# Gate and up tiles 6 to 21 of a feed-forward layer in pairs, by seven half-size products

## The chip, the cores and the metric

The kernel runs on one core of a Trainium2 chip. The metric is the device time of one execution in microseconds; the runs shown are whole executions, the profile is one more of them, with every instruction recorded.

A core has five engines that run their own queues in order and wait for one another by semaphores: PE (TensorE, matmuls; its weight loads are listed as PEld), DVE (VectorE), ACT (ScalarE), POOL (GpSimd) and SP (SyncE, which issues most DMAs here).

## The reference

Two transformer blocks in float32, one after the other, 512 tokens of width 1024. The change lies in the feed-forward layer that ends the first block:

```
h = rms_norm(x, pre_ffn_norm)
f = (silu(h @ w_ffn_gate) * (h @ w_ffn_up)) @ w_ffn_down     # 1024 -> 2816 -> 1024
x = x + rms_norm(f, post_ffn_norm)
```

## The kernel before

Activations are held transposed: a tile has 128 features as partitions and 512 tokens as columns. The width 1024 is 8 tiles (KD), the inner width 2816 is 22 (KF); `n` numbers these 22. The weights `w_fgu` hold the gate and the up tile of each n one after the other, so row 2n is gate n and row 2n + 1 is up n; each row is 128 x 1024: 8 blocks of 128 columns, one for each k of the contraction.

float32 products are made of three matmuls in float32r. `pair` splits a tile into a high part (ACT, L135, a cast) and a low part (DVE, L139, what the cast lost), and `mm3` (L207 to L209) multiplies high by high, high by low and low by high into one PSUM bank. `wload` has SP load 128 x 1024 of weights into a buffer of a ring (`RAW`, names `wr`; three buffers) and makes two pairs of 512 columns of it (`wh`, `wl`). `lin` is one output tile: 8 k times `mm3`, 24 matmuls of 512 columns. `evac` (L370, DVE) takes the bank to SBUF and multiplies it by R, the reciprocal norm of each token, since `hs` holds the tokens times the gain, not yet normed. `repair` is `pair` of a tile that is then let go (`prh`, `prl`).

SBUF tiles come from 84 slots of 128 x 512 (and 14 half slots). `A` takes the slot at the head of a line of free slots and `free` puts one at its end: a slot that is taken late after it was let go costs no wait, and what a new tile waits for is the last reader of the slot's former tile.

The loop over n: the gate and up tiles of n = 0 to 2 are made by `first_halves` while the norm is still being made; from n = 3 on by two `lin` each. Then silu on the gate tile (ACT), the product with the up tile (DVE, L924) and `repair` of it, whose pair goes into the list `hid`. After n = 10 the down projection of these 11 tiles is made into `fs` (8 tiles, `fs_first`), and after n = 21 `down_last` adds that of the other 11: 6 output tiles by `lin` with 11 k, the last two by `last_halves`, in two halves of 256 columns, so that the norm of the first half can begin while the second half is multiplied.

The kernel is written as one program for all engines; a scheduler orders the instructions of each engine's queue at build time, by its own estimate of times and with the slots as constraints. So the order on each engine is not the order of the source.

Of the kernel before, what the change touches and what calls it, by code (L numbers as in the profile page):

```python
# [10 lines left out]
F32 = mybir.dt.float32  # L11
# [3 lines left out]
ALU = mybir.AluOpType  # L15
# [43 lines left out]
def two_blocks(ctx: ExitStack, tc: tile.TileContext, d, dbg=None):  # L59
    nc = tc.nc  # L60
    V, S, G, PE = nc.vector, nc.scalar, nc.gpsimd, nc.tensor

    NSLOT, NHALF = 84, 14
    cst = ctx.enter_context(tc.tile_pool(name="cst", bufs=1))
    ar = ctx.enter_context(tc.tile_pool(name="ar", bufs=1))
    pp = ctx.enter_context(tc.tile_pool(name="pp", bufs=1, space=bass.MemoryType.PSUM))
# [8 lines left out]
    def A(name, dt=F32, cols=T):  # L75
        if cols > 256 or len(spare_half) < 3:
            i = spare.popleft()
            low[0] = min(low[0], len(spare))
            ap = ar.tile([P, T], dt, tag="slot%d" % i, name=name)[:, :cols]
            owner[id(ap)] = (spare, i, ap, name)  # L80
        else:
            i = spare_half.popleft()
            ap = ar.tile([P, 256], dt, tag="half%d" % i, name=name)[:, :cols]
            owner[id(ap)] = (spare_half, i, ap, name)
        return ap

    def free(*xs):
        for x in xs:
            if isinstance(x, (tuple, list)):
                free(*x)  # L90
            else:
                home, i = owner.pop(id(x))[:2]
                home.append(i)

    def ring(pool, n, shape, name, dt=F32):
        tiles = [pool.tile(shape, dt, name="%s%d" % (name, i)) for i in range(n)]
        at = [0]

# [17 lines left out]

    MM, AT, OP, ST = (lambda: bank("mm")), (lambda: bank("at")), (lambda: bank("op")), (lambda: bank("st"))
    share(mm=(0, 1, 2, 3, 4), at=(5, 6), op=(7,), st=(5, 6))
    RAW = ring(ar, 3, [P, 1024], "wr")
    SMALL = ring(cst, 32, [P, 8], "sm")  # L120
    RTOK = ring(cst, 16, [P, NT], "rtok")

# [82 lines left out]
    def mm3(ps, a, b, first, last):  # L205
        (ah, al), (bh, bl) = a, b
        r = PE.matmul(ps, lhsT=ah, rhs=bh, start=first, stop=False)  # L207
        PE.matmul(ps, lhsT=ah, rhs=bl, start=False, stop=False)  # L208
        PE.matmul(ps, lhsT=al, rhs=bh, start=False, stop=last)  # L209
        return r.ins  # L210

    def lin(w, n, hs, cols=T, k0=0, after=None):

        kt = len(hs)
        ps = MM()
        wt = wtile(w, n, kt, k0)
        for k in range(kt):
            r = mm3(ps[:, :cols], wpart(wt, k), hs[k], k == 0, k == kt - 1)
            if k == 0 and after:
                order(r, after)  # L220
        free(wt[1])
        return ps
# [114 lines left out]
    def vcol(name, i=0, n=1):  # L337
        return vec[:, VOFF[name] + i:VOFF[name] + i + n]
# [28 lines left out]
    def evac(ps, name, Rt, scale=None, cols=T):  # L367
        o = A(name)
        if scale is None:
            V.tensor_tensor(o[:, :cols], ps[:, :cols], Rt[:, :cols], ALU.mult)  # L370
        else:
            V.scalar_tensor_tensor(o[:, :cols], ps[:, :cols], scale, Rt[:, :cols], ALU.mult, ALU.mult)
        return o

    def repair(x, cols=T, eh=None, el=None):

        p = pair("pr", x[:, :cols], None, cols, eh, el)
        free(x)
        return p

    HALVES = (slice(0, 256), slice(256, 512))

    def last_halves(ns, wts, hs, out, after=None, stat=None, at=(0, 0)):

# [521 lines left out]
    def fs_first(n, ps):  # L908
        fs[n] = A("f")
        S.copy(fs[n], ps)  # L910
# [4 lines left out]
        V.tensor_tensor(fs[n][:, c], fs[n][:, c], ps, ALU.add)  # L915
        st.add(fs[n][:, c], c)

    for n in range(KF):
        if n < 3:
            zg, zu = firsts[2 * n], firsts[2 * n + 1]  # L920
        else:
            zg, zu = [evac(lin(d["w_fgu"], 2 * n + j, hs), "z", R) for j in range(2)]
        act("silu", zg, zg, AF.Silu)
        V.tensor_tensor(zu, zu, zg, ALU.mult)  # L924
        free(zg)
        hid.append(repair(zu))
        if n == HF - 1:
            for m in range(KD):
                fs_first(m, lin(d["w_fd"], m, hid))
            free(hid)  # L930
            hid = []
    free(hs, R)

    def down_last(w, hid, out, after, ahead=None, nl=2, stat=None, at=(0, 0)):
        for n in range(KD - nl):
            both(out)(n, lin(w, n, hid, k0=HF))
        wl2 = [wtile(w, n, KF - HF, HF) for n in range(KD - nl, KD)]
        if ahead:
            ahead()
        last_halves(range(KD - nl, KD), wl2, hid, out, after, stat, at)  # L940
        free(hid)
# [5 lines left out]
            v2ws.extend(wload(d["w2V"][0, :, k * T:(k + 2) * T]))  # L947
        qkws.extend(wtile(d["w2T"], n, KD) for n in (0, 4))

    down_last(d["w_fd"], hid, fs_add, st.done, ahead, 2, st, (5, 14))  # L950
    hs, sth = chained(xs, "attn_norm", DM, post_norm(fs, st, "post_ffn", xs))


# [550 lines left out]
```

## Time and profile before

| | |
|---|---|
| three runs | 1758.90, 1757.07, 1757.78 us (median 1757.78) |
| profiled execution | 1757.92 us; span of its instructions 1755.9 us |
| granted TensorE clock, mean | 0.994 |
| busy in the span | PE 98%, PEld 84%, DVE 61%, ACT 47%, POOL 5% |
| DMA | 169.97 MB, 97 GB/s on average |

A row of groups reads: line, engine, operation, output<-inputs, shapes, count | busy us, mean ns of one | idle time of the engine just before them, and what ended most of it. A row of the timeline reads: start in us from the span's start, length in us, engine, line, operation; "x4" merges four that follow each other, and [..] is the idle time before, with what ended it. Matmuls, DVE and ACT instructions overlap at their ends, so what one costs in a full queue is the distance between starts, which is shorter than its length. DMA rows give KB each and the median us from issue to landing.

### The profile page before, as it was taken

To read this page: it belongs to the slowest core of one execution; us is meant where nothing else is said; L and a number is where in the kernel's file an instruction comes from. 1 tells how busy PE (TensorE), PEld (TensorE's weight loads), DVE (VectorE), ACT (ScalarE), POOL (GpSimd) and SP (SyncE) were. 2 spreads that over 40 slices of the span, in tenths; PEclk is the share of its full clock that TensorE was granted. 3 is DMA by queue.
4 is the path that set the end of the run, shared out by engine and by line. 5 is a ranking of instruction groups with operands and counts; after the bars stand their busy time and mean duration, and the time that the engine had idled before them with its cause. 6 is when DMAs were issued, how large, how long until landed. Compare 5 with 4: busy or idle time off the path is not lost.

```text
span 1755.9 us, 24063 instructions
## 1 busy us (share of the span) xinstructions
PE 1718.4 (98%) x9039; PEld 1469.4 (84%) x9039; DVE 1079.4 (61%) x2103; ACT 830.9 (47%) x1695; POOL 90.5 (5%) x109
## 2 busy tenths in 40 slices
PE   8999999999999999999999999999999999999998
PEld 7888888878889888888897887887898988888887
DVE  7447863587757543344557656787756587547752
ACT  6534543565544432323425656687525454324442
POOL 1000000100004000000012000000210200000000
PEclk9999999999999999999999999999999999999999
DMA  6212251223440423422413443433314133432221
GB/s 225 83 48 72 83 162 41 61 61 104 156 156 5 152 79 90 120 77 81 146 46 95 121 109 103 126 102 108 128 44 137 47 102 88 126 96 84 74 83 49
DMA packets 60915, 169.97 MB, mean 97 GB/s; under 512 B 7616, under 2 KB 16512, under 8 KB 60800
## 3 DMA queue, kind: packets, MB, share of 16 engines
q1 hardware_dynamic: 60528, 168.24, 32.1%
q8 instruction: 71, 1.16, 0.3%
q14 instruction: 44, 0.36, 0.1%
q10 hardware_dynamic: 144, 0.14, 0.0%
q0 software_dynamic: 128, 0.07, 0.0%
HBM read 151.64 MB, written 2.10 MB: 88 GB/s over the span
## 4 chain that ended last, share of the span: by engine, by line
PE 87%; DVE 5%; ACT 3%; DMA 2%; issue 2%; POOL 1%; SPq 0%; POOLq 0%; DVEq 0%; ACTq 0%
PE bank L207 27%; PE bank L208 27%; PE bank L209 27%; PE bank L1086 1%; DVE wl L139 1%; DVE hl L141 1%; PE bank L729 1%; DVE f L861 1%; DMA wr<-w_mq 1%; PE bank L1045 0%; ACT wh L135 0%; PE bank L1046 0%; DVE x L862 0%; PE bank L293 0%; DMA mem<-memT 0%
## 5 line engine op out<-in xcount | busy, mean ns | idle before, releaser
L139 DVE TENSOR_TENSOR wl<-wr,wh 128x512 fp32r<-128x512 f32 (+2 forms) x568 | 375.6, 678 | 302.5 <-ACT wh L135 171.2
L135 ACT CAST wh<-wr 128x512 fp32r<-128x512 f32 (+2 forms) x568 | 333.9, 608 | 462.8 <-PE bank L209 144.6
L207 PE MATMUL bank<-hh,wh 128*128 128x512 f32 (+1 forms) x1380 | 504.9, 368 | 7.5 <-ACT wh L135 5.7
L209 PE MATMUL bank<-hh,wl 128*128 128x512 f32 (+1 forms) x1380 | 505.3, 367 | 0.0
L208 PE MATMUL bank<-hl,wh 128*128 128x512 f32 (+1 forms) x1380 | 504.7, 366 | 0.0
L207 PEld LDWEIGHTS bank<-hh,wh 128*128 128x128 f32 x1380 | 260.6, 189 | 48.8 <-ACT wh L135 6.4
L209 PEld LDWEIGHTS bank<-hh,wl 128*128 128x128 f32 x1380 | 260.7, 189 | 41.7 <-DVE wl L139 0.7
L208 PEld LDWEIGHTS bank<-hl,wh 128*128 128x128 f32 x1380 | 260.8, 189 | 40.5
L208 PE MATMUL bank<-prl,wh 128*128 128x512 f32 (+1 forms) x471 | 171.5, 364 | 0.0
L209 PE MATMUL bank<-prh,wl 128*128 128x512 f32 (+1 forms) x471 | 171.4, 364 | 0.0
L207 PE MATMUL bank<-prh,wh 128*128 128x512 f32 (+1 forms) x471 | 171.1, 365 | 0.0
L207 PEld LDWEIGHTS bank<-prh,wh 128*128 128x128 f32 x471 | 88.8, 189 | 14.2
L208 PEld LDWEIGHTS bank<-prl,wh 128*128 128x128 f32 x471 | 88.9, 189 | 14.1
L209 PEld LDWEIGHTS bank<-prh,wl 128*128 128x128 f32 x471 | 88.8, 189 | 13.9
L254 POOL TENSOR_TENSOR rtok<-sm,minus_half 128x2 f32<-128x2 f32 (+1 forms) x20 | 16.4, 822 | 1271.4 <-DVE sm L253 1271.4
L208 PE MATMUL bank<-wl,hh 128*128 128x512 f32 (+1 forms) x192 | 71.4, 374 | 0.4 <-DVE wl L139 0.4
L209 PE MATMUL bank<-wh,hl 128*128 128x512 f32 (+1 forms) x192 | 70.3, 374 | 0.0
L207 PE MATMUL bank<-wh,hh 128*128 128x512 f32 (+1 forms) x192 | 69.6, 377 | 0.0
L270 ACT ACTIVATE sq<-x 128x256 f32<-128x256 f32 (+1 forms) x88 | 36.8, 425 | 42.2 <-DVE x L1332 38.4
L137 ACT ACTIVATE hh<-x,vec 128x256 fp32r<-128x256 f32 (+1 forms) x72 | 37.7, 527 | 36.4 <-DVE x L862 14.1
L281 POOL TENSOR_TENSOR sq<-sq 128x256 f32<-128x256 f32 x56 | 46.1, 827 | 95.1 <-ACT sq L270 92.7
L141 DVE SCALAR_TENSOR_TENSOR hl<-x,vec,hh 128x256 fp32r<-128x256 f32 (+1 forms) x72 | 46.2, 658 | 5.4 <-ACT hh L137 5.4
(368 smaller groups left out, 2761.9 us busy)
## 6 DMA issues: line engine op xcount, KB each, us to landing
wr<-w_fgu SPq DMA_DIRECT2D x44, 512.0 KB, 3.7
wr<-w_up SPq DMA_DIRECT2D x44, 512.0 KB, 3.6
wr<-w1T SPq DMA_DIRECT2D x16, 512.0 KB, 3.5
wr<-w_gate SPq DMA_DIRECT2D x16, 512.0 KB, 3.8
wr<-w_fd SPq DMA_DIRECT2D x16, 512.0 KB, 3.6
wr<-w2T SPq DMA_DIRECT2D x16, 512.0 KB, 3.9
wr<-w_dn SPq DMA_DIRECT2D x16, 512.0 KB, 3.6
wr<-w1K SPq DMA_DIRECT2D x12, 512.0 KB, 4.3
```

What stands on the lines that cost most here:

```text
L135: r = S.copy(hi, src) if eh is S else V.tensor_copy(hi, src)
L137: r = S.activation(hi, src, AF.Copy, scale=scale)
L139: q = el.tensor_tensor(lo, src, f(hi), ALU.subtract)
L141: q = V.scalar_tensor_tensor(lo, src, scale, f(hi), ALU.mult, ALU.subtract)
L207: r = PE.matmul(ps, lhsT=ah, rhs=bh, start=first, stop=False)
L208: PE.matmul(ps, lhsT=ah, rhs=bl, start=False, stop=False)
L209: PE.matmul(ps, lhsT=al, rhs=bh, start=False, stop=last)
L270: S.activation(q[:, :w], src, AF.Square)
L281: self.eadd.tensor_tensor(acc, acc, q[:, :w], ALU.add)
L729: PE.transpose(tp[:, i * P:(i + 1) * P], ps_tiles[i][:, b * P:(b + 1) * P], C("ident"))
L861: r = V.scalar_tensor_tensor(fs[k][:, c], fs[k][:, c], vcol(gain, k), st.R[:, c], ALU.mult, ALU.mult)
L1086: PE.matmul(z[:, (b2 - b) * P:w], lhsT=lt, rhs=part[:, :T - b2 * P], start=False, stop=False)
```

## The change

Tiles n = 0 to 5 stay as they are. From n = 6 on, two n are taken together: the two gate tiles by one call of `seven`, then the two up tiles by another, 16 calls in all. A call sees the two tiles of weights as a 2 x 2 block matrix (output tile a or b, first or second 4 k), and the tokens as 2 x 2 blocks too (first or second 4 k, first or second 256 columns), and makes the four blocks of the output from 7 products of half size in place of 8: each product is 4 k times `mm3` on 256 columns, 12 matmuls. In the order of the program the seven stationary operands are a11, a12, s2, s3, s1, s4 and a22, with sums of blocks of weights s1 = a22 + a21, s3 = a11 + a21 (by the blocks' names in the code), s2 = s1 + a11, s4 = s2 + a12; they are called product 1 to 7 below. s2 and s4 are made by DVE. s1 and s3 are made by DMA: SP loads one block into a slot `s`, and POOL issues a DMA that adds the other block to it.

The combinations of token blocks (`ts`) are made once, by `normed_sums`, from tokens that are already normed (`ns`), which are therefore made anew; `hs` and R are let go. The results of the products are joined by DVE: u2, u3, u4 (L290 of the new kernel) and four writes into the two output tiles (L1035), all of 256 columns; u1 is copied by ACT. `evac` is not needed there.

The down projection goes in three passes: after n = 5 (6 k), after n = 13 (8 k, with 8 additions on DVE), and `down_last` (8 k), whose last three tiles go in halves. The ring RAW has four buffers, and there are 82 slots. During the calls all 8 PSUM banks go round.

```diff
-    NSLOT, NHALF = 84, 14
+    NSLOT, NHALF = 82, 14
...
-    RAW = ring(ar, 3, [P, 1024], "wr")
+    RAW = ring(ar, 4, [P, 1024], "wr")
...
+    def seven_sums(b0, b1):
+
+        h0, h1 = HALVES
+        u, v = A("t12"), A("t34")
+        V.tensor_tensor(u[:, h0], b0[:, h1], b0[:, h0], ALU.subtract)
+        V.tensor_tensor(u[:, h1], b1[:, h1], u[:, h0], ALU.subtract)
+        V.tensor_tensor(v[:, h0], b0[:, h1], b1[:, h1], ALU.subtract)
+        V.tensor_tensor(v[:, h1], b1[:, h0], u[:, h1], ALU.subtract)
+        return repair(u), repair(v)
+
+    def seven(w, na, nb, hs, ts, out):
+        half = len(hs) // 2
+        n_ = half * P
+        h0, h1 = HALVES
+        raws = []
+        for n in (na, nb):
+            raw = RAW()
+            nc.sync.dma_start(raw[:, :2 * n_], w[n, :, 0:2 * n_])
+            raws += [raw[:, :n_], raw[:, n_:2 * n_]]
+        a11, a12, a21, a22 = raws
...
+        def ps_for(a, b):
+            ps = MM()
+            for k in range(half):
+                mm3(ps[:, :256], (a[0][:, k * P:(k + 1) * P], a[1][:, k * P:(k + 1) * P]), b(k),
+                    k == 0, k == half - 1)
+            free(a)
+            return ps[:, :256]
+
+        def plus(ps, x, op=ALU.add):
+            o = A("u", F32, 256)
+            V.tensor_tensor(o[:, :256], ps, x[:, :256], op)
+            return o
+
+        def summed(x, y, op):
+            o = A("s", F32, n_)
+            V.tensor_tensor(o[:, :n_], x, y, op)
+            return o
+
+        sums = []
+        for n, c, m, e in ((nb, slice(n_, 2 * n_), nb, slice(0, n_)), (na, slice(0, n_), nb, slice(0, n_))):
+            o = A("s", F32, n_)
+            nc.sync.dma_start(o[:, :n_], w[n, :, c])
+            G.dma_start(o[:, :n_], w[m, :, e], accum_op=ALU.add)
+            sums.append(o)
+        s1, s3 = sums
+        s2 = summed(s1[:, :n_], a11, ALU.add)
+        p1 = ps_for(pair("w", a11, None, n_), lambda k: cols(hs[k], h0))
+        u1 = A("u", F32, 256)
+        S.copy(u1[:, :256], p1)
+        out(na, ps_for(pair("w", a12, None, n_), lambda k: cols(hs[half + k], h0)), u1[:, :256], h0)
+        u2 = plus(ps_for(pair("w", s2[:, :n_], None, n_), lambda k: cols(ts[k][0], h1)), u1, ALU.subtract)
...
+        w1 = pair("w", s1[:, :n_], None, n_)
+        w3 = pair("w", s3[:, :n_], None, n_)
+        u3 = plus(ps_for(w3, lambda k: cols(ts[k][1], h0)), u2)
+        p5 = ps_for(w1, lambda k: cols(ts[k][0], h0))
+        out(nb, p5, u3[:, :256], h1)
+        u4 = plus(p5, u2)
+        s4 = summed(s2[:, :n_], a12, ALU.add)
+        w4 = pair("w", s4[:, :n_], None, n_)
+        out(na, ps_for(w4, lambda k: cols(hs[half + k], h1)), u4[:, :256], h1, ALU.subtract)
+        out(nb, ps_for(pair("w", a22, None, n_), lambda k: cols(ts[k][1], h1)), u3[:, :256], h0)
...
-    for n in range(KF):
-        if n < 3:
-            zg, zu = firsts[2 * n], firsts[2 * n + 1]
-        else:
-            zg, zu = [evac(lin(d["w_fgu"], 2 * n + j, hs), "z", R) for j in range(2)]
+    def gated(zg, zu):
         act("silu", zg, zg, AF.Silu)
         V.tensor_tensor(zu, zu, zg, ALU.mult)
         free(zg)
         hid.append(repair(zu))
-        if n == HF - 1:
+
+    G1, G2 = 6, 14
+    for n in range(G1):
+        if n < 3:
+            gated(firsts[2 * n], firsts[2 * n + 1])
+        else:
+            gated(*[evac(lin(d["w_fgu"], 2 * n + j, hs), "z", R) for j in range(2)])
+
+    def normed_sums(xs, gain, hs, R):
+        ns, ts = [None] * KD, []
+        for k in range(KD // 2):
+            b = []
+            for j in (k, k + KD // 2):
+                x = A("n")
+                V.scalar_tensor_tensor(x, xs[j], vcol(gain, j), R, ALU.mult, ALU.mult)
+                ns[j] = pair("n", x)
+                b.append(x)
+            ts.append(seven_sums(*b))
+            free(b)
+        return ns, ts
+
+    ns, ts = normed_sums(xs, "pre_ffn", hs, R)
+    free(hs, R)
+    for m in range(KD):
+        fs_first(m, lin(d["w_fd"], m, hid))
+    free(hid)
+    hid = []
+
+    def seven_pair(w, na, nb):
+        o = {na: A("z"), nb: A("z")}
+
+        def out(n, ps, u, c, op=ALU.add):
+            V.tensor_tensor(o[n][:, c], ps, u, op)
+
+        seven(w, na, nb, ns, ts, out)
+        return o[na], o[nb]
+
+    share(mm=range(8), at=(), op=(), st=())
+    for n in range(G1, KF, 2):
+        zg = seven_pair(d["w_fgu"], 2 * n, 2 * n + 2)
+        for g, u in zip(zg, seven_pair(d["w_fgu"], 2 * n + 1, 2 * n + 3)):
+            gated(g, u)
+        if n + 2 == G2:
             for m in range(KD):
-                fs_first(m, lin(d["w_fd"], m, hid))
+                ps = lin(d["w_fd"], m, hid, k0=G1)
+                V.tensor_tensor(fs[m], fs[m], ps, ALU.add)
             free(hid)
             hid = []
-    free(hs, R)
+    free(ns, ts)
...
-    down_last(d["w_fd"], hid, fs_add, st.done, ahead, 2, st, (5, 14))
+    down_last(d["w_fd"], hid, fs_add, st.done, ahead, 3, st, (5, 14))
```

The order on DVE, before, around the gate and up tiles of n = 12 (z_6582 is its gate, z_6617 its up tile; the last z is the gate of n = 13):

```order
L370 TENSOR_TENSOR z_6582<-bank4_68,R_5139 128x512
L139 TENSOR_TENSOR wl_6890<-wr2_74,wh_6889 128x512
L370 TENSOR_TENSOR z_6617<-bank5_69,R_5139 128x512
L139 TENSOR_TENSOR wl_6894<-wr2_74,wh_6893 128x512
L924 TENSOR_TENSOR z_6617<-z_6617,z_6582 128x512
L139 TENSOR_TENSOR prl_6622<-z_6617,prh_6621 128x512
L139 TENSOR_TENSOR wl_6931<-wr0_72,wh_6930 128x512
L370 TENSOR_TENSOR z_6658<-bank0_64,R_5139 128x512
```

And in the changed kernel, from product 4 of the 6th call (up tiles of n = 10 and 11) to product 7, with the weights of the 7th call (gate tiles of n = 12 and 13) among them: s_6906 is its s1, s_6909 its s3, s_6912 its s2, s_7004 its s4:

```order
L290 TENSOR_TENSOR u_6837<-bank6_70,u_6815 128x256
L295 TENSOR_TENSOR s_6912<-s_6906,wr2_74 128x512
L1035 TENSOR_TENSOR z_6753<-bank7_71,u_6837 128x256
L290 TENSOR_TENSOR u_6852<-bank7_71,u_6815 128x256
L139 TENSOR_TENSOR wl_6968<-s_6906,wh_6967 128x512
L295 TENSOR_TENSOR s_7004<-s_6912,wr2_74 128x512
L139 TENSOR_TENSOR wl_6972<-s_6909,wh_6971 128x512
L1035 TENSOR_TENSOR z_6752<-bank0_64,u_6852 128x256
L139 TENSOR_TENSOR wl_6950<-s_6912,wh_6949 128x512
L1035 TENSOR_TENSOR z_6753<-bank1_65,u_6837 128x256
```

Where DVE had two low parts of weights for each z, it now has sums and low parts of sums of the next call between the joins of this one, and one that waits for an adding DMA (s_6912) stands ahead of four joins.

POOL's order around the layer, before (the instructions of the two norms, one after the other):

```order
L281 TENSOR_TENSOR sq<-sq 128x256 x2
L254 TENSOR_TENSOR rtok_111<-sm_87,minus_half 128x2
L254 TENSOR_TENSOR rtok_112<-sm_88,minus_half 128x2
L862 TENSOR_TENSOR x<-x,f 128x256
L281 TENSOR_TENSOR sq<-sq 128x256
```

And after:

```order
L361 TENSOR_TENSOR sq<-sq 128x256 x2
L334 TENSOR_TENSOR rtok_112<-sm_88,minus_half 128x2
L302 DMA s<-w_fgu 128x512 x32
L334 TENSOR_TENSOR rtok_113<-sm_89,minus_half 128x2
L940 TENSOR_TENSOR x<-x,f 128x256
```

The 32 adding DMAs stand between the norm ahead of the layer and the one behind it, with nothing else among them.

DVE's order at the end of the first block, before (z_6073 is the up tile of n = 10, and the rows behind it are weights of the down projection):

```order
L370 TENSOR_TENSOR z_6038<-bank4_68,R_5139 128x512
L139 TENSOR_TENSOR wl_6283<-wr1_73,wh_6282 128x512
L139 TENSOR_TENSOR wl_6288<-wr2_74,wh_6287 128x384
L370 TENSOR_TENSOR z_6073<-bank5_69,R_5139 128x512
L924 TENSOR_TENSOR z_6073<-z_6073,z_6038 128x512
L139 TENSOR_TENSOR prl_6078<-z_6073,prh_6077 128x512
```

And after, behind product 7 of the 8th call (bank7), with the two up tiles of n = 12 and 13:

```order
L1035 TENSOR_TENSOR z_7041<-bank7_71,u_7125 128x256
L1035 TENSOR_TENSOR z_7040<-bank6_70,u_7140 128x256
L139 TENSOR_TENSOR wl_7294<-wr1_73,wh_7293 128x512
L998 TENSOR_TENSOR z_7041<-z_7041,z_6903 128x512
L998 TENSOR_TENSOR z_7040<-z_7040,z_6902 128x512
L139 TENSOR_TENSOR prl_7187<-z_7041,prh_7186 128x512
L139 TENSOR_TENSOR wl_7328<-wr2_74,wh_7327 128x512
L139 TENSOR_TENSOR prl_7181<-z_7040,prh_7180 128x512
```

One z, one product and one low part have become two each, with two low parts of weights among them.

More of the change, by code (lines that the diff above doesn't have):

```diff
@@ L248, in tok_step @@
         return mm3(ps, (h[0][:, q], h[1][:, q]), w, first, last)
+    HALVES = (slice(0, 256), slice(256, 512))
+    def seven_sums(b0, b1):
[6 more added lines that the diff above has]
+        return repair(u), repair(v)
@@ new lines, in seven, with cols @@
+    def seven(w, na, nb, hs, ts, out):
[8 more added lines that the diff above has]
+        a11, a12, a21, a22 = raws
+        def cols(p, c):
+            return p[0][:, c], p[1][:, c]
+        def ps_for(a, b):
[26 more added lines that the diff above has]
+        u2 = plus(ps_for(pair("w", s2[:, :n_], None, n_), lambda k: cols(ts[k][0], h1)), u1, ALU.subtract)
+        free(u1)
+        w1 = pair("w", s1[:, :n_], None, n_)
+        free(s1)
+        w3 = pair("w", s3[:, :n_], None, n_)
+        free(s3)
+        u3 = plus(ps_for(w3, lambda k: cols(ts[k][1], h0)), u2)
+        p5 = ps_for(w1, lambda k: cols(ts[k][0], h0))
+        out(nb, p5, u3[:, :256], h1)
+        u4 = plus(p5, u2)
+        free(u2)
+        s4 = summed(s2[:, :n_], a12, ALU.add)
+        free(s2)
+        w4 = pair("w", s4[:, :n_], None, n_)
+        free(s4)
+        out(na, ps_for(w4, lambda k: cols(hs[half + k], h1)), u4[:, :256], h1, ALU.subtract)
+        free(u4)
+        out(nb, ps_for(pair("w", a22, None, n_), lambda k: cols(ts[k][1], h1)), u3[:, :256], h0)
+        free(u3)
@@ L379, in repair @@
         return p
-    HALVES = (slice(0, 256), slice(256, 512))
     def last_halves(ns, wts, hs, out, after=None, stat=None, at=(0, 0)):
@@ L926, in two_blocks @@
         hid.append(repair(zu))
-        if n == HF - 1:
+    G1, G2 = 6, 14
[34 more added lines that the diff above has]
+        if n + 2 == G2:
             for m in range(KD):
-                fs_first(m, lin(d["w_fd"], m, hid))
+                ps = lin(d["w_fd"], m, hid, k0=G1)
+                V.tensor_tensor(fs[m], fs[m], ps, ALU.add)
             free(hid)
             hid = []
-    free(hs, R)
+    free(ns, ts)
+    share(mm=(0, 1, 2, 3, 4, 5), at=(6, 7), op=(), st=(6, 7))
     def down_last(w, hid, out, after, ahead=None, nl=2, stat=None, at=(0, 0)):
+        k0 = KF - len(hid)
         for n in range(KD - nl):
-            both(out)(n, lin(w, n, hid, k0=HF))
-        wl2 = [wtile(w, n, KF - HF, HF) for n in range(KD - nl, KD)]
+            both(out)(n, lin(w, n, hid, k0=k0))
+        wl2 = [wtile(w, n, KF - k0, k0) for n in range(KD - nl, KD)]
         if ahead:
```

## The prediction

> **What bounds the kernel now.** I read the page's busy times and slices first, then a window over the first feed-forward layer, then starts of matmuls one by one.
>
> ```profile
> span 1755.9 us, 24063 instructions
> ...
> PE 1718.4 (98%) x9039; PEld 1469.4 (84%) x9039; DVE 1079.4 (61%) x2103; ACT 830.9 (47%) x1695; POOL 90.5 (5%) x109
> ...
> DMA  6212251223440423422413443433314133432221
> GB/s 225 83 48 72 83 162 41 61 61 104 156 156 5 152 79 90 120 77 81 146 46 95 121 109 103 126 102 108 128 44 137 47 102 88 126 96 84 74 83 49
> ```
>
> The window holds gate and up from n = 3 on and the whole down projection but its end. Columns: busy time and count of each engine, granted clock, DMA share, GB/s.
>
> ```profile
> core 0: us, PE busy (x) PEld busy (x) DVE busy (x) ACT busy (x) POOL busy (x), PEclk, DMA share, GB/s
> 583.00:914.00 331.00, 331.00 (x1533) 277.12 (x1532) 146.71 (x245) 109.40 (x193) 2.81 (x4) 1.00 0.32 96
> 583.00:648.00 65.00, 65.00 (x292) 53.94 (x291) 32.03 (x51) 21.99 (x37) 0.00 (x0) 1.00 0.29 90
> ```
>
> PE has no gap in 331 us at full clock, and DVE works 44% of them. So the stage is worth what its matmuls cost at their start-to-start distance; a busy time of 0.39 us is pipelined and no price. From the timeline of PE, the first and the last of 22 matmuls of 512 columns, and of 24 of 256:
>
> ```profile
> 600.07 0.39 PE L207 MATMUL bank<-hh,wh 128*128 128x512 f32 x1
> ...
> 604.83 0.39 PE L207 MATMUL bank<-hh,wh 128*128 128x512 f32 x1
> ```
>
> ```profile
> 905.71 0.28 PE L207 MATMUL bank<-prh,wh 128*128 128x256 f32 x1
> ...
> 908.46 0.28 PE L209 MATMUL bank<-prh,wl 128*128 128x256 f32 x1
> ```
>
> 4.76 / 21 = 0.2267 us for 512 columns, 2.75 / 23 = 0.1196 for 256; I take 0.120.
>
> **The change, part by part.** *Matmuls.* Two tiles by plain products are 48 matmuls of 512 columns, 10.88 us; a call of `seven` is 7 x 12 of 256, 84 x 0.120 = 10.08 us. The order of instructions has 774 fewer of 512 and 1356 more of 256 (12 of these from the third tile in halves at the end): -175.5 + 162.7 = -12.8 us. One product is 12 x 0.120 = 1.44 us. All of this is on the path.
>
> *DVE.* Its distances, from groups and merged rows (a merged row's count and length; the last one's own duration is taken off):
>
> ```profile
> L139 DVE TENSOR_TENSOR wl<-wr,wh 128x512 fp32r<-128x512 f32 x106 | 72.0, 690 | 106.2 <-PE bank L208 52.6 <-ACT wh L135 49.5 <-ACT z L170 1.6
> L915 DVE TENSOR_TENSOR f<-f,bank 128x256 f32<-128x256 f32 x16 | 6.2, 416 | 17.1 <-PE bank L209 17.1
> ```
>
> ```profile
> 567.57 3.69 DVE L139 TENSOR_TENSOR wl<-wr,wh 128x512 fp32r<-128x512 f32 x6
> ...
> 565.18 1.41 DVE L901 TENSOR_TENSOR z<-bank,R 128x256 f32<-128x256 f32 x4
> ```
>
> (3.69 - 0.69) / 5 = 0.60 us for 512 columns, (1.41 - 0.42) / 3 = 0.33 for 256. A call needs 7 low parts, 2 sums, and one pair's mult and low part twice: 11 x 0.60 + 7 x 0.33 = 8.9 us, of PE's 10.08. The two tiles took 4 + 2 + 2 = 8 x 0.60 = 4.8 before. So DVE goes from 44% to 88%: no new bound, but it can make up only 1.2 us of lateness in a call. ACT has 7 casts, silu, cast and a copy, below 10 x 0.62 = 6.2 us:
>
> ```profile
> L135 ACT CAST wh<-wr 128x512 fp32r<-128x512 f32 x101 | 60.9, 621 | 102.8 <-PE bank L209 47.5 <-PE bank L208 41.9 <-DMA wr<-w_fgu 11.3
> ```
>
> *normed_sums.* 24 DVE instructions of 512 columns and 16 of 256, 19.7 us (the scalar_tensor_tensor counted like the others), beside n = 3 to 5 and the first down pass, whose 144 + 144 matmuls take 65.3 us. The window 583 to 648 has 33 us of idle DVE; without that cover it would cost its 19.7. Taken as nothing.
>
> *The f sums of the second pass* (8 DVE additions, 4.8 us) stand beside 192 matmuls, 43.5 us: nothing. *At the two joints* (after n = 13 and n = 21) the down pass needs the last hid after only 6 k, 18 x 0.2267 = 4.1 us. DVE's rows behind the last product are two z, five of 512 and the low part: 0.66 + 3.0 + 0.69 = 4.35. Each joint costs 0.3, together 0.6. *A fourth raw buffer* shifts loads in other stages; taken as 0, with 3 us to either side as bounds, about half of
>
> ```profile
> PE bank L207 <- ACT wh L135: 6.0, 2, 5.7
> ```
>
> *The adding DMAs.* A call moves 2 MiB where two tiles moved 1, so 96 GB/s become some 208; the first slice, 225 GB/s at a DMA share of 6 tenths, shows that this goes. What they cost is a chain: a slot comes free, SP loads 256 KB, POOL adds 256 KB, DVE sums. The rows on its links (KB each, median us from issue to landing):
>
> ```profile
> wr<-w_out SPq DMA_DIRECT2D x16, 256.0 KB, 2.9
> ...
> x<-xT SPq DMA_DIRECT2D x16, 256.0 KB, 4.1
> ...
> pos<-pos POOLq DMA_DIRECT2D x4, 16.0 KB, 4.4
> ```
>
> No DMA of before adds. From below its landing is 2.9 (as if SP had issued it); from above 4.4 + 2.9 = 7.3 (the second read comes on top). I take 4.4, the one row of that queue. SP's load is between 2.9 and 4.1, loads standing alone and in a crowd; I take 3.5. The chain is 7.9 us.
>
> When is its slot free? At the 7th call (n = 12, 13) 82 slots less 8 x, 8 f, 32 of ns and ts, 12 of hid and 2 z leave 20, so `s` takes the slot let go 20 frees earlier: of the 22 since the 6th call began, the third, the high part of a12, read last by product 2. The weights of product 3 are due 7 products later, 10.1 us. In between: 7.9, and on DVE from `s2` to its low part 4 x 0.60 + 3 x 0.33 + 0.69 = 4.1. PE waits 12.0 - 10.1 = 1.9 us. Meanwhile DVE stands at `s2` with `z`, `u` and the next weights behind it; SP's waiting load has raw loads behind it that are due a call or more later, and POOL's queue holds nothing else here: nothing for either. The other tight calls, in the same way: the 8th has 8 products, 11.5, for 7.9 + 3.4 = 11.3; the 6th (a slot of `gated`) 11.9 for 7.9 + 3.2; the 2nd (slots of hid, three in a row, 0.7 more) 13.0 for 7.9 + 0.7 + 4.3. They just fit; the 3rd to 5th have 13.0 or more. The second block repeats the first: 2 x 1.9 = 3.8.
>
> Sum: -12.8 + 0.6 + 3.8 = -8.4. The profiled execution took 1757.9 us (span 1755.9 and 2.0 around it), the median of the runs is 1757.8: 1749.5.
>
> **A rule that speaks against it.** PE loads weights once a matmul, so halving the columns doubles the loads. The row of a load, columns as above:
>
> ```profile
> L209 PEld LDWEIGHTS bank<-hh,wl 128*128 128x128 f32 x363 | 68.4, 188 | 11.8
> ```
>
> The Trainium skill, TensorE: Matmul & The Clock Gate, Part 3 (what overlaps and what doesn't), says that a weight load overlaps a matmul in flight only where the row group differs. All loads here use the whole array. By that rule 0.19 us would stand ahead of each matmul, and a call would lose. The trace disagrees: 0.2267 and 0.1196 leave no room for a load of 0.188.
>
> **The rivals.**
> *The chain is longer (slower).* With 10 us in place of 7.9 (the adding DMA lands after 6.5) a block waits 2.0 at the 2nd call, 1.3 at the 6th, 4.0 at the 7th and 1.9 at the 8th: 9.2, twice 18.4, and 1757.9 - 12.8 + 0.6 + 18.4 = 1764. It decides from a chain of about 9.2 us on. For it: no row shows an add, and traffic doubles. Against it: the 4.4 was measured in the fullest slice.
> *All of it is hidden.* With both landings at 2.9 the chain is 5.8 and no call waits: 1757.9 - 12.2 = 1745.7. The Trainium skill, DMA: Bandwidth & Descriptors, Anatomy of one DMA, has 2.0 us plus bytes over 436 GB/s for a DMA of this path; by it an add is an estimated 2.6 us, and this rival would hold. The only row, 4.4 for 16 KB, is above it.
> *DVE becomes the bound.* Work on POOL slows DVE in the trace: the same instruction takes 0.48 alone and 0.96 beside POOL.
>
> ```profile
> 537.45 0.48 DVE L861 SCALAR_TENSOR_TENSOR f<-f,vec,R 128x256 f32<-128x256 f32 x1 [1.34 <-ACT R L307]
> ...
> 542.05 0.96 DVE L861 SCALAR_TENSOR_TENSOR f<-f,vec,R 128x256 f32<-128x256 f32 x1
> ...
> 541.87 0.86 POOL L862 TENSOR_TENSOR x<-x,f 128x256 f32<-128x256 f32 x1 [0.41 <-ACT sq L270]
> ...
> L479 POOL DMA_DIRECT2D pos<-pos x4 | 2.2, 551 | 0.8 <-POOLq L1495 0.8
> ```
>
> If each adding DMA stops DVE for its issue of 0.55 us, a call needs 8.9 + 1.1 = 10.0 of 10.08, and with half a product of DVE's own waiting a call 10.7: 16 x 0.6 = 10 us come back, 1757.9 - 12.2 + 10 = 1755.7, no change. Bounds 0 and 10. DVE ran nothing beside those four issues, so no row tells. The Trainium skill, SBUF — State Buffer, Who interferes with whom, has tensor_tensor share only the read port with GpSimd while descriptors need the write port, which speaks against this; that no run here shows.
> *Weight loads bind at 256 columns.* With 0.188 between matmuls a call costs 84 x 0.308 = 25.9 against 48 x 0.415 = 19.9: 16 x 6 = 96 us slower, 1854. The rule weighed above points here. The rows above exclude it but for a surprise.
> That the change does not do what it says is out: the order holds 32 DMAs on POOL and the counts above.
>
> **How the numbers follow.** The sum 0.50, within 1746 to 1753; all hidden 0.15; the longer chain 0.18; DVE the bound 0.15; weight loads 0.02. A measurement of this kernel tells 0.2%, 3.5 us, from no change, so faster is below 1754.3. Faster: 0.48 of the sum, all hidden, 0.06 of DVE the bound and 0.01 of the chain: 0.70. Slower: 0.13 of the chain, 0.02 of DVE the bound, the loads: 0.17. The same: the rest, 0.13. The range goes from the hidden case less 1 us of the raw buffer to most of the longer chain: 1744.5 to 1762.
>
> **What would show it.** PE's starts 0.120 apart through all calls; the landing of the adding DMAs near 4.4; idle time of DVE ahead of `s2` put down to a DMA; PE waiting for low parts of weights at the 7th and 15th call and hardly elsewhere; DVE near 88% busy between the products. I am wrong if adding DMAs land later than 6 us, if DVE's 512-column instructions come more than 0.60 apart beside POOL's issues, or if PE waits at most calls.

## The result and the profile after

The changed kernel takes 1771.13 us (median of 6 runs, 1768.6 to 1774.28) against 1757.83 us of the kernel before beside it: a ratio of 1.0076, 95% interval 1.0063 to 1.0089. It is slower by 13.3 us; 1749.5 was forecast, and the time lies outside the range of 1744.5 to 1762. The profiled execution took 1770.41 us, its span is 1768.6.

The page of the changed kernel, the lines that answer to those of before:

```profile
span 1768.6 us, 25739 instructions
...
PE 1716.1 (97%) x9621; PEld 1492.6 (84%) x9621; DVE 1165.8 (66%) x2311; ACT 867.8 (49%) x1775; POOL 122.5 (7%) x141
```

The span is 12.7 us longer, though PE's busy time is 2.3 us shorter: PE waits more. The stretches of the layer (columns as in the prediction's windows): plain tiles and the first down pass, most of the 1st to 8th call, the second down pass, most of the 9th to 16th:

```profile
588.00:653.00 65.00, 65.00 (x289) 53.79 (x288) 43.10 (x78) 28.21 (x51) 3.65 (x4) 1.00 0.38 106
653.00:743.00 90.00, 81.94 (x652) 80.07 (x651) 62.95 (x125) 37.94 (x71) 10.62 (x12) 0.98 0.58 148
743.00:787.00 44.00, 44.00 (x207) 36.86 (x206) 23.21 (x40) 14.06 (x24) 1.77 (x2) 1.00 0.44 130
787.00:877.00 90.00, 82.68 (x655) 80.87 (x654) 65.35 (x128) 38.66 (x73) 12.30 (x14) 0.98 0.65 170
```

In the two stretches without calls PE has no gap; in both stretches with calls it idles for 7 to 8 us and the granted clock drops to 0.98. DVE is busy 70 to 73% there, which speaks against DVE as the bound (e2 below tests it). The waits of 640 to 900 us (us in total, times, longest):

```profile
PE bank L207 <- ACT wh L135: 14.0, 9, 2.7
PE bank L209 <- DVE wl L139: 1.3, 6, 0.3
...
DVE s L295 <- DMA s<-w_fgu: 34.0, 13, 5.3
```

PE waits for weights, and for their casts on ACT (14.0 us) much more than for DVE's low parts (1.3). DVE stands 34 us at `s2`, and what it waits for there is the adding DMA. Sorted by call, PE's gaps stand in the 5th to 8th and in the 13th to 16th, mostly ahead of product 3; in the 13th they are 0.4 us in all.

A measure for all runs below: a norm ends by PE transposing the reciprocal norm (`bank<-con,rtok`). From the first such row of the norm ahead of the layer to that of the norm behind it, before 536.63 to 908.58, after 540.77 to 921.77:

```profile
536.63 0.38 PE L301 MATMUL bank<-con,rtok 128*128 128x128 f32 x2
...
908.58 0.38 PE L301 MATMUL bank<-con,rtok 128*128 128x128 f32 x2
```

```profile
540.77 0.38 PE L381 MATMUL bank<-con,rtok 128*128 128x128 f32 x2
...
921.77 0.38 PE L381 MATMUL bank<-con,rtok 128*128 128x128 f32 x2
```

So read, the profiled spans fall into three parts (us):

| kernel | ahead | layer | behind | median us | ratio to before, interval |
|---|---|---|---|---|---|
| before | 536.6 | 372.0 | 847.3 | 1757.8 | |
| changed | 540.8 | 381.0 | 846.8 | 1771.1 | 1.0076, 1.0063 to 1.0089 |
| e1 POOL loads | 541.5 | 374.1 | 845.7 | 1759.6 | 1.0019, 1.0007 to 1.0031 |
| e2 all sums on DVE | 539.8 | 358.6 | 846.0 | 1749.1 | 0.9955, 0.9939 to 0.9971 |
| e3 no adds | 540.3 | 358.6 | 844.9 | 1746.4 | 0.9936, 0.9919 to 0.9952 |
| e4 before, four raw buffers | 540.2 | 372.0 | 841.8 | 1755.9 | 0.9992, 0.9982 to 1.0003 |
| e5 four own slots | 540.1 | 358.5 | 846.7 | 1747.9 | 0.9938, 0.9919 to 0.9957 |
| e6 own slots, POOL loads | 539.6 | 358.5 | 846.9 | 1746.2 | 0.9928, 0.9907 to 0.9949 |
| e7 three passes | 541.5 | 374.7 | 856.5 | 1769.9 | 1.0070, 1.0047 to 1.0093 |
| e8 e2 with three raw buffers | 540.8 | 358.6 | 844.8 | 1742.7 | 0.9912, 0.9892 to 0.9933 |
| e9 two own slots | 540.1 | 390.2 | 846.3 | 1778.3 | 1.0121, 1.0105 to 1.0136 |
| e10 e5 with three raw buffers | 536.3 | 358.9 | 846.6 | 1743.0 | 0.9920, 0.9906 to 0.9933 |
| e11 e2 again | 541.6 | 358.6 | 848.3 | 1748.9 | 0.9955, 0.9942 to 0.9967 |
| e12 e8 again | 535.7 | 358.6 | 845.0 | 1741.9 | 0.9917, 0.9904 to 0.9931 |
| e13 changed, three raw buffers | 538.2 | 384.5 | 845.1 | 1769.3 | 1.0074, 1.0058 to 1.0089 |
| e14 order of casts | 540.7 | 377.8 | 849.7 | 1766.2 | 1.0053, 1.0037 to 1.0070 |
| e15 e14 with POOL loads | 540.9 | 372.4 | 844.5 | 1759.6 | 1.0014, 1.0003 to 1.0024 |

The layer is 9.0 us longer than before, and 22.4 us longer than in the versions without waits in the calls (358.5 to 358.9 in eight profiles). Of the 22.4, 15.3 are the idle time above, and by estimate 3.4 come from two stretches of 3.4 us at half clock that follow waits (the last section shows one); the rest is not itemised. Each row is one profiled execution, and the three parts vary from one execution to the next (the same kernel, e8 and e12, has 540.8 and 535.7 ahead of the layer), so differences of a few us between rows with waits are weak evidence.

**One wait in full**, that of the 7th call. SP's, POOL's, DVE's, ACT's and PE's timelines of the changed kernel:

```profile
705.52 0.33 SPq L301 DMA_DIRECT2D s<-w_fgu  x1
...
713.38 0.33 SPq L273 DMA_DIRECT2D wr<-w_fgu  x1
713.80 0.86 SPq L301 DMA_DIRECT2D s<-w_fgu  x2
```

```profile
718.17 1.77 POOL L302 DMA_DIRECT2D s<-w_fgu  x2 [7.38 <-DMA s<-w_fgu]
```

```profile
722.37 0.69 DVE L295 TENSOR_TENSOR s<-s,wr 128x512 f32<-128x512 f32 x1 [4.09 <-DMA s<-w_fgu]
```

```profile
722.42 0.62 ACT L135 CAST wh<-s 128x512 fp32r<-128x512 f32 x1 [5.80 <-DMA s<-w_fgu]
724.37 1.66 ACT L135 CAST wh<-s 128x512 fp32r<-128x512 f32 x3 [1.33 <-DMA s<-w_fgu]
```

```profile
710.11 0.28 PE L209 MATMUL bank<-nh,wl 128*128 128x256 f32 x1
712.37 0.39 PE L207 MATMUL bank<-prh,wh 128*128 128x256 f32 x1 [1.98 <-ACT wh L135]
...
722.78 0.28 PE L209 MATMUL bank<-nh,wl 128*128 128x256 f32 x1
725.56 0.53 PE L207 MATMUL bank<-prh,wh 128*128 128x256 f32 x1 [2.50 <-ACT wh L135]
725.89 0.42 PE L208 MATMUL bank<-prl,wh 128*128 128x256 f32 x1
```

By the order of the slots, that of `s1` is let go when product 2 of the 6th call ends, at 710.4. Its load goes out 3.4 us later (4.1 in the text of e1 below, which counted from the start of the product's last matmuls), 0.4 us behind a raw load, ahead of which SP had issued nothing since 705.85. That raw load waited for the last reader of its buffer, which was DVE's `s4` of the 6th call; and DVE had been late there because `s2` of the 6th call had waited for its own adding DMA. SP's wait, and DVE's two sums of the 6th call:

```profile
SPq L273 <- DVE s L295: 7.5, 1, 7.5
```

```profile
710.98 0.69 DVE L295 TENSOR_TENSOR s<-s,wr 128x512 f32<-128x512 f32 x1 [2.75 <-DMA s<-w_fgu]
...
712.63 0.68 DVE L295 TENSOR_TENSOR s<-s,wr 128x512 f32<-128x512 f32 x1
```

So a late sum makes the next one late: without these 2.75 us the raw load could have gone out at about 710.6 (an estimate from these rows), close to when the slot came free. From SP's issue of the load to POOL's of the add are 4.4 us, from there to `s2` 4.2. `s2` is ready at 723.06, but its cast is the second of three that begin at 724.37: ACT's queue has the casts in this order, and s_6909, the s3 of product 4, lands later than the s1 (names as in the order shown above for DVE):

```
L135 CAST wh_6967<-s_6906 128x512
L135 CAST wh_6971<-s_6909 128x512
L135 CAST wh_6949<-s_6912 128x512
```

### The profile page after: what moved, and what is told of

It reads as the page before. It is cut to its first block, busy times and chain, and to the rows that moved or that the text cites. A ratio compares the mean times of both kernels' runs of the same rounds, so it can differ in the third digit from the quotient of the medians.

```text
span 1768.6 us, 25739 instructions
## 1 busy us (share of the span) xinstructions
PE 1716.1 (97%) x9621; PEld 1492.6 (84%) x9621; DVE 1165.8 (66%) x2311; ACT 867.8 (49%) x1775; POOL 122.5 (7%) x141
## 4 chain that ended last, share of the span: by engine, by line
PE 83%; DVE 7%; DMA 4%; ACT 3%; issue 2%; POOL 0%; SPq 0%; POOLq 0%; DVEq 0%; ACTq 0%
PE bank L207 26%; PE bank L208 25%; PE bank L209 25%; DMA s<-w_fgu 3%; DVE wl L139 1%; PE bank L1207 1%; DVE hl L141 1%; PE bank L807 1%; DVE f L939 1%; ACT wh L135 1%; PE bank L1166 1%; DMA wr<-w_mq 1%; PE bank L1167 1%; DVE prl L139 0%; PE bank L373 0%
## 5 line engine op out<-in xcount | busy, mean ns | idle before, releaser
L207 PE MATMUL bank<-hh,wh 128*128 128x512 f32 (+1 forms) x1124 | 407.6, 364 | 10.3 <-ACT wh L135 6.0
L209 PE MATMUL bank<-hh,wl 128*128 128x512 f32 (+1 forms) x1124 | 406.7, 363 | 1.0 <-DVE wl L139 1.0
L208 PE MATMUL bank<-hl,wh 128*128 128x512 f32 (+1 forms) x1124 | 405.7, 362 | 0.0
L207 PE MATMUL bank<-prh,wh 128*128 128x256 f32 (+1 forms) x729 | 245.1, 339 | 12.6 <-ACT wh L135 12.6
L208 PE MATMUL bank<-prl,wh 128*128 128x256 f32 (+1 forms) x729 | 244.8, 337 | 0.0
L209 PE MATMUL bank<-prh,wl 128*128 128x512 f32 (+1 forms) x729 | 243.8, 338 | 1.0 <-DVE wl L139 0.9
L209 PEld LDWEIGHTS bank<-hh,wl 128*128 128x128 f32 x1124 | 213.0, 190 | 33.0 <-DVE wl L139 1.2
L207 PEld LDWEIGHTS bank<-prh,wh 128*128 128x128 f32 x729 | 139.7, 192 | 27.8 <-ACT wh L135 14.0
L209 PEld LDWEIGHTS bank<-prh,wl 128*128 128x128 f32 x729 | 138.9, 191 | 16.1 <-DVE wl L139 2.0
L208 PEld LDWEIGHTS bank<-prl,wh 128*128 128x128 f32 x729 | 139.8, 192 | 14.0
```

## The experiments

**Theories after the result.** *Queue*: loads of `s` stand in SP's queue behind raw loads that wait for a buffer. *Slots*: the slot at the head of the line is let go too late. *Length*: the adding DMAs are too slow in themselves. *DVE*: DVE can't do its work in the time of a call.

**e1, POOL loads** (outside SP's queue):

```diff
-            nc.sync.dma_start(o[:, :n_], w[n, :, c])
-            G.dma_start(o[:, :n_], w[m, :, e], accum_op=ALU.add)
-            sums.append(o)
+            G.dma_start(o[:, :n_], w[n, :, c])
+            sums.append((o, w[m, :, e]))
+        for o, src in sums:
+            G.dma_start(o[:, :n_], src, accum_op=ALU.add)
+        sums = [o for o, src in sums]
```

> The 32 loads of s are issued by POOL in place of SP, ahead of the adding DMAs; nothing else is changed. Queue theory: in calls 5, 7 and 8 of a block the load of s goes out 2.6, 4.1 and 4.0 us after its slot is free, because a load of raw weights stands ahead of it in SP's queue and waits for a buffer; DVE then stands at s2 and lets slots and buffers go late, which brings the 6th call's wait too. Without SP's queue most of the 22.5 us of PE's waits in the 16 calls go: 4 to 8 us are left, and the time is 1754 to 1758. Length theory: the chain load, add, sum is itself too long (9 us in place of 7.9); POOL's issue of 0.87 us for each load makes it longer by 1 us, the waits stay or grow, 1771 to 1776. DVE theory (DVE cannot do its work in a call): no change, 1771.

The layer takes 374.1 us, 6.9 less, and the wait of the 5th call is gone; the 6th still waits 3.0 and the 14th 3.8 us, and the time, 1759.6, is above the 1754 to 1758 of the queue theory. So SP's queue was a part, and less than forecast. POOL's rows show what is left, the two loads of the 6th call and those of the 7th:

```profile
700.94 0.58 POOL L301 DMA_DIRECT2D s<-w_fgu  x1 [8.88 <-DVE z L1000]
703.42 0.58 POOL L301 DMA_DIRECT2D s<-w_fgu  x1 [1.90 <-DVE prl L139]
...
708.17 1.45 POOL L301 DMA_DIRECT2D s<-w_fgu  x2
```

The slots of the 6th call's sums are let go by DVE's product of the z tiles and its low part, late. Those of the 7th go out at 708.17, where PE ends product 2 of the 6th call (708.14), as the order of the slots says.

The same run tells about the add (L301 loads, L304 adds):

```profile
L301 POOL DMA_DIRECT2D s<-w_fgu x32: 548/580/889, 620.8 to 855.6; - x32
...
DMA to landing us min/median/max: 3.1/4.9/6.5
```

```profile
L304 POOL DMA_DIRECT2D s<-w_fgu x32: 847/888/1217, 626.0 to 861.0; - x32
...
DMA to landing us min/median/max: 3.6/4.6/7.6
```

Here an adding DMA lands no later than a plain one of the same queue. That doesn't hold throughout: in e6 below, where POOL issues both too, the loads (first) land earlier than the adds:

```profile
DMA to landing us min/median/max: 2.8/3.8/7.6
```

```profile
DMA to landing us min/median/max: 3.9/5.9/10.5
```

**e2, all sums on DVE**, and **e3, no adds** (it drops only the line with `accum_op`); the edit of e2:

```diff
-        for n, c, m, e in ((nb, slice(n_, 2 * n_), nb, slice(0, n_)), (na, slice(0, n_), nb, slice(0, n_))):
-            o = A("s", F32, n_)
-            nc.sync.dma_start(o[:, :n_], w[n, :, c])
-            G.dma_start(o[:, :n_], w[m, :, e], accum_op=ALU.add)
-            sums.append(o)
+        for x, y in ((a22, a21), (a11, a21)):
+            sums.append(summed(x, y, ALU.add))
```

> All four sums of a call are made by DVE from the raw buffers; the 64 DMAs of s are gone. DVE gets 2 more sums a call, by 0.60 us 10.1 us of PE's 10.08. Queue and length theory: what waited for the adding DMAs is gone, PE waits under 0.5 us in most calls, 1749 to 1758. DVE theory: DVE was already the limit, 1.2 us more in each of 16 calls, 1780 to 1790.

> The adding DMAs are left out (s1 and s3 hold one block of weights in place of a sum of two); SP's loads of s stay where they are. The chain is shorter by POOL's issue and the add, about 5 us. Queue and length theory: the waits of 1.3 to 2.9 us are all shorter than that, PE waits under 4 us in all, 1750 to 1756. If the shortage of slots delays the weights themselves, or DVE is the limit, the waits stay: 1768 to 1772.

Both leave no wait in the calls; e2, two stretches that hold most of the calls and some of the down pass behind each block of them:

```profile
653.00:743.00 90.00, 90.00 (x712) 88.20 (x711) 79.53 (x154) 43.50 (x80) 0.00 (x0) 1.00 0.32 104
787.00:863.00 76.00, 76.00 (x613) 74.93 (x612) 69.74 (x137) 40.66 (x74) 0.00 (x0) 1.00 0.32 105
```

DVE does two sums more in each call and PE has no gap: the DVE theory is out. e3's time, 1746.4, lies below what was forecast for it. The layer is 13.4 us shorter than before. The DMA traffic is lower too (105 GB/s for 148 to 170), which e5 excludes as the cause.

**e4, the kernel before with four raw buffers and 82 slots:**

```diff
-    NSLOT, NHALF = 84, 14
+    NSLOT, NHALF = 82, 14
-    RAW = ring(ar, 3, [P, 1024], "wr")
+    RAW = ring(ar, 4, [P, 1024], "wr")
```

> The kernel before with four raw buffers and 82 slots, no call of seven. If the 4.1 us that the changed kernel is late at the start of the layer come from the order that the fourth buffer gives, 1761 to 1763; if they come from elsewhere, 1757 to 1759.

It is 3.6 us late at the layer and 5.5 faster behind it: no change in all, and 1755.9 lies below both forecasts.

**e5, own slots** for s1 and s3, taken out of the line while the calls last, and **e6**, the same with POOL's loads:

```diff
-            o = A("s", F32, n_)
+            o = turns()
...
-        free(s1)
...
-        free(s3)
...
+    turns = ring_of([A("s") for i in range(4)])
...
-    free(ns, ts)
+    free(ns, ts, turns.tiles)
```

> s1 and s3 go round four slots that are taken out of the line of free slots for the length of the calls, so the slot of a sum was last read two calls earlier; SP still loads them. Slots theory (the sums start late because the slot at the head of the line was let go late, in the 6th call by DVE's work on the z tiles): the chain can start a call earlier, of the 22.5 us of waits under 4 are left, 1751 to 1755. Queue theory (the loads stand in SP's queue behind raw loads that wait for a buffer): SP's queue is as it was, 12 to 22 us of waits stay, 1761 to 1771.

> Own slots as in the run before, and POOL loads them as in the first run: neither the line of slots nor SP's queue is left in the chain. If these two are all of the waits, under 3 us of waits, 1748 to 1753. If the chain's length alone makes PE wait, or the four slots that the weights lack cost as much, the waits stay above 10 us, 1758 or more.

In e5 no wait of PE is left, at 193 and 170 GB/s and with adds that land later than in the changed kernel (the first fence is e5, its two stretches and its DMA rows; the second the changed kernel):

```profile
653.00:743.00 90.00, 90.00 (x713) 88.30 (x713) 73.40 (x142) 43.63 (x79) 12.24 (x14) 1.00 0.73 193
787.00:863.00 76.00, 76.00 (x614) 75.00 (x613) 64.67 (x126) 41.74 (x75) 8.11 (x10) 1.00 0.63 170
...
s<-w_fgu SPq DMA_DIRECT2D x32, 256.0 KB, 3.2
s<-w_fgu POOLq DMA_DIRECT2D x32, 256.0 KB, 5.9
```

```profile
s<-w_fgu SPq DMA_DIRECT2D x32, 256.0 KB, 3.8
s<-w_fgu POOLq DMA_DIRECT2D x32, 256.0 KB, 5.2
```

The chain is as long as ever; it starts early enough (in the 7th call at 690.77 in place of 713.80). That rules out length by itself and traffic. SP's queue no longer matters then: e6 has the same layer. Both times, 1747.9 and 1746.2, lie a little below their forecasts. But e5 doesn't weigh slots against SP's queue, as its text means to: with the own slots the scheduler also put the loads further ahead in that queue (13 raw loads of the calls go out ahead of the 7th call's sums, 16 in the changed kernel). What the queue alone is worth is told by e1.

**e7, three passes**, so that fewer slots hold hid:

```diff
-    G1, G2 = 6, 14
+    G1, G2 = 6, (12, 18)
...
-        if n + 2 == G2:
+        if n + 2 in G2:
...
-                ps = lin(d["w_fd"], m, hid, k0=G1)
+                ps = lin(d["w_fd"], m, hid, k0=n + 2 - len(hid))
```

> The changed kernel with the down projection after n = 11 and n = 17 in place of after n = 13 alone: at most 12 slots of hid in place of 16, and 8 more additions on DVE beside matmuls. Slots theory: the two tightest calls of a block, the 7th and 8th, are gone, and the 5th and 6th have as many slots as before; what they waited, 1.3 and 2.1 to 4 us of a block, stays in each of two and a half blocks: 8 to 12 us of 22.5 us, 1759 to 1763. If traffic or DVE make the waits, as many as before or more: 1770 to 1776.

The layer is 6.3 us shorter, but what follows is 9.7 us longer. The last pass has only 4 k for each tile, and PE now waits for the norm behind it, where the changed kernel waits 1.1 us:

```profile
PE bank L373 <- DVE sq L361: 3.9, 2, 2.6
PE bank L381 <- POOL rtok L334: 2.4, 1, 2.4
```

One wait of 2.6 us of these still lies in the layer as measured here, so they are a part of the 9.7; the rest isn't traced. The profiled execution is also the slowest of the five, 4.6 us above their median. The calls moved as forecast, roughly; the time, 1769.9, did not: it is that of the changed kernel.

**e9, two own slots** in place of e5's four:

> Own slots as before, but two in place of four: the load of a sum waits until the same sum of the call before has been split, which is about when product 4 of that call starts, 8.6 to 10 us before the weights of product 3 of its own call are due. The chain as measured (load 3.2 to 3.8, handover and add 5.2 to 5.9, then s2, cast and low part about 2) is 10.5 to 12 us. If what decides is the distance from the slot's release to the due product against the chain's length, PE now waits 1 to 3 us in nearly every call, 16 to 45 us in all, 1765 to 1793. If the chain were shorter than that distance, or the tight slots of the weights were the cause and not the sums', no wait: 1746 to 1750.

The layer takes 390.2 us, 31.7 above that without waits, of which 20.2 are idle time of PE, and the time is within the first forecast. In size this fits the forecast, that the distance from a slot's release to the due product decides, set against the chain's length. Call by call it doesn't show it: PE waits in seven calls, not in nearly every one, and the longest wait stands ahead of product 1 of the 6th call, whose cast on ACT stands behind that of a sum that had not landed:

```profile
711.64 0.58 PE L207 MATMUL bank<-nh,wh 128*128 128x256 f32 x1 [4.87 <-ACT wh L135]
```

**e8, e10 to e12: three raw buffers and 84 slots** in e2 and e5.

> All four sums on DVE, with three raw buffers and 84 slots in place of four and 82. DVE reads a11 and a12 of a call late, for s2 and s4, so a raw buffer is held for most of a call. If three buffers do: 1747 to 1751, as with four. If raw loads wait for a buffer: PE waits for the first weights of calls, 1755 to 1765.

> Four own slots, with three raw buffers and 84 slots. If the fourth raw buffer is worth what all-DVE with three seemed to gain, 1741 to 1744; if the two are alike, 1746 to 1750; if raw loads wait for a buffer, above 1750.

> The all-DVE version with four raw buffers and 82 slots once more, beside the one with three and 84 on the same chip. The two profiled spans were 1744.4 and 1744.2 us, so the raw buffers should make no difference: 1745 to 1749, and a ratio within 0.002 of the other's.

> All-DVE with three raw buffers and 84 slots, beside the other. As its span was the same: 1745 to 1749. If its lower times (1742.7 against 1749.1, on two occasions) were real, 1742 to 1744 with the other 5 to 6 us above.

e8 came below its forecasts (1742.7), e10 in its first case (1743.0). e11 and e12, on one chip: 0.9955 and 0.9917, 7 us apart, much as e2 and e8; of the 9.2 us between the spans 5.9 stand ahead of the layer and none in it. That the two spans of e2 and e8 agreed had misled me: e8's profiled execution happened to lose some 5 us ahead of the layer that e12's did not. In all of these runs three buffers go with 84 slots and four with 82, so the two are not told apart.

**e13, three raw buffers in the changed kernel:**

> The changed kernel with three raw buffers and 84 slots, the rest as it is. Of the 13 us that it is slower, 4.2 stand ahead of the layer, in a stage whose order the fourth buffer changes (the kernel before with four buffers is also 3.6 late there, but has it back at the end). If the fourth buffer costs the changed kernel those 4 and the waits in the calls stay: 1765 to 1768. If two more slots and three buffers also change the calls: 1755 to 1763 if the slots decide, above 1772 if the raw loads, which stand ahead of the sums' loads in SP's queue, wait longer.

2.6 us are gained ahead of the layer and 3.5 lost in it; the time, 1769.3, is that of the changed kernel. SP's rows around the 7th call show the loads of `s` again right behind raw ones:

```profile
706.78 3.32 SPq L273 DMA_DIRECT2D wr<-w_fgu  x2
710.19 0.86 SPq L301 DMA_DIRECT2D s<-w_fgu  x2
```

**e14, order of casts**, and **e15**, the same with POOL's loads:

```diff
-        u2 = plus(ps_for(pair("w", s2[:, :n_], None, n_), lambda k: cols(ts[k][0], h1)), u1, ALU.subtract)
+        w2 = pair("w", s2[:, :n_], None, n_)
+        first = made[0]
+        u2 = plus(ps_for(w2, lambda k: cols(ts[k][0], h1)), u1, ALU.subtract)
...
         w3 = pair("w", s3[:, :n_], None, n_)
+        order(made[0], first)
```

> ACT's cast of s2 is put ahead of its cast of s3; nothing else changes in the program. In the 7th, 8th, 15th and 16th call ACT's queue has s1, s3, s2, though product 3 needs s2 and product 4 needs s3: s2 is ready at 723.06 us in the 7th call, its cast starts at 724.89, behind that of s3, whose adding DMA lands 2 us after the first one's. If this order is part of the waits: those four calls wait 2.66, 1.13, 1.58 and 2.13 us less 1.7 to 2.3 each, about 1 us instead of 7.5, and without the half clock that follows two of them the layer is 7 to 11 us shorter, 370 to 374 us from norm to norm, 1760 to 1765. If it is not (the next cast or DVE's low part is late as well): 378 to 381, 1768 to 1772.

> The order of casts as in the run before, and all loads of s by POOL as in the first run. If the queue of SP and the order on ACT are separate causes they add up: what is left is the 6th and 14th call, whose slots DVE lets go late, 5 to 8 us of waits, the layer 364 to 367 us, 1751 to 1755. If POOL's loads had already removed what the order of casts costs: 372 to 375 as with POOL's loads alone, 1759 to 1762.

e14 gains 3.2 us in the layer, less than half of what was forecast: the waits of the 7th, 15th and 16th call shrink, that of the 8th grows to 2.5 us. e15's layer is 1.7 us below e1's, and its time is the same as e1's, 1759.6: its second case came, and the two causes don't simply add up. So of 22.4 us the order of casts and SP's queue together are 8.6 (381.0 to 372.4). The other 13.9 go when the sums have slots of their own, or need none (e2). In e1 and e15 most of PE's waits that are left stand in the 6th and 14th call, whose slots DVE lets go late; no run changed that release alone.

## Why the prediction was wrong

*The step that failed is the adding-DMA chain*: 3.8 us forecast, 22.4 measured. Its sum for the 7th call has the right form, but that the wait came out near (1.9 forecast, 2.7 measured from start to start) is luck, since the terms were others. It let the load go out when the slot is free; SP's queue held it for 3.4 us more. The prediction asked what stands behind the waiting load, not what it stands behind. It took 7.9 us from SP's issue to `s2`; it was 8.6 here and 10.1 in the 5th call (SP 686.04, `s2` 696.19). It took 4.1 us from there, for DVE to the low part; here 3.2 passed, and PE waited for ACT's cast of `s2`, which stood behind that of `s3` and so behind the second adding DMA. In all 15.2 us from 710.4 to 725.56, not 12.0; the wait is only 2.7 because the 6th call had waited 2.1 already. Calls that "just fit", and the 5th, which had time to spare, did not: eight wait, not two. And the prediction took each call by itself, while a late sum makes the next late: DVE stands at `s2` with the z tiles and raw halves behind it, whose slots and buffers the next chain needs, as the rows of the 6th call show.

*The landing.* 4.4 us was forecast for the add, 5.2 measured, 3.5 and 3.8 for SP's load. The Trainium skill, DMA: Bandwidth & Descriptors, Anatomy of one DMA, gives an estimated 2.6 us for 256 KB on POOL's path; the traces lie above it, plain loads from POOL with 2.8 us at the least and a median of 3.8 (e6), adds with 3.6 at the least (e1).

*Right:* the matmuls, at a distance of 0.120 us throughout; their sum and the joints, -12.2 forecast, -13.4 in the versions without waits (the joints cost nothing; 0.6 I can't place). `normed_sums` and the f sums hidden: 65.00 of 65.00 and 44.00 of 44.00 us. DVE's price was near and a little high: e2's two sums more would make 10.1 of 10.08 us by the prediction's figures, and yet they fit; from 653 to 733 us, almost all of it calls, DVE is busy 72.8 of 80 us there, 91%.

*The fourth raw buffer*, taken as 0 within 3: in the kernel before (e4) and in the changed one (e13) right for the whole time, though something is lost ahead of the layer: twelve profiles with four buffers have 539.6 to 541.6 us there; of five with three, four have 535.7 to 538.2 and one 540.8. Where the waits are gone four buffers, with two slots fewer, cost 7 us (e11 and e12, on one chip), so the bounds were too narrow. e5 and e10 point the same way, 5 us by the medians and 3 by the ratios, but on two chips and with intervals that overlap.

*The rivals.* The longer chain came nearest, with 18.4 us forecast for it and 22.4 measured, 1764 and 1771. But its cause isn't what was found: the chain was 8.6 to 10.1 us where traced, about the 9.2 of its condition, and by e5 a chain as long leaves no wait if it starts early. It also had waits in the 2nd call, where there are none. No rival had a late start. All hidden gives the time that e2, e3 and e5 show (1745.7 forecast, 1746.4 to 1749.1), though not by landings of 2.9 us. DVE as the bound is out by e2, weight loads as the bound by the distance of 0.120 us.

## What to carry over

When a product waits for a chain of DMAs, count from when the buffer at the chain's head is let go to when the product is due, and add what stands ahead in every in-order queue on the way: the loads ahead in SP's queue, the casts ahead on ACT. If that fits by less than a few us, give the chain buffers of its own: four slots here were worth 22 us, two were not enough. And look for the plain way first: the two sums by DVE, which seemed to have no room, are as fast as four own slots, both with three raw buffers: 1742 us (e12, 0.9917, 0.9904 to 0.9931) and 1743 (e10, 0.9920, 0.9906 to 0.9933), the shortest times of all.

## What the hardware showed

- A DMA that adds takes 0.89 us of POOL's issue in place of 0.58 (e1). In landing it was no slower than a plain one of the same queue in e1 (4.6 and 4.9 us), and slower in e6 (5.9 and 3.8); what makes the difference was not tried. The loads that SP issues landed after 3.8 (changed kernel) and 3.2 (e5).
- A wait of PE can be paid twice. After that of 2.5 us in the 7th call, the clock is halved for 3.4 us (the matmul rows at 725.56 lie 0.22 to 0.33 apart, not 0.12). The wait of 2.0 us in the 6th call was not followed by half clock (first row; columns as in the other windows, the granted clock is third from the end):

```profile
712.40:715.80 3.40, 3.29 (x25) 3.08 (x26) 3.40 (x8) 2.89 (x6) 0.00 (x0) 1.00 0.59 162
...
725.60:729.00 3.40, 3.40 (x16) 3.40 (x17) 3.40 (x8) 2.00 (x5) 0.00 (x0) 0.51 0.88 277
729.00:733.00 4.00, 4.00 (x35) 4.00 (x35) 3.64 (x7) 1.50 (x3) 1.78 (x2) 0.99 0.45 75
```

The Trainium skill, TensorE: Matmul & The Clock Gate, Part 1, has the clock fall after an idle window of about 3.4 us; here 2.5 us were enough. The length alone doesn't tell, though: in e13 a wait of 2.0 us that ended at 811.86 was followed by half clock, and in e7 one of 2.5 us that ended at 711.88 was not (e13 first):

```profile
811.90:815.30 3.40, 2.71 (x11) 2.42 (x12) 3.40 (x7) 2.18 (x4) 0.00 (x0) 0.50 0.52 154
```

```profile
711.90:715.30 3.40, 3.32 (x24) 3.04 (x25) 3.40 (x8) 2.83 (x6) 0.00 (x0) 1.00 0.33 93
```

- POOL's DMA issues did not slow DVE: its 512-column rows stand 0.60 us apart in e5, beside 1.77 us of issue in a call, as in e2 without any.
